# A Fourier stage whose standing operands are cut into two pieces of 64 columns, with two stores requested behind the loads

## The chip, the cores and the metric

The kernel runs on one core of a Trainium2 chip. The metric is the device time of one execution in microseconds (us); before the change it is 971.48 us, the median of three runs (970.88, 971.48 and 973.24). The core's engines are TensorE (PE in the profile, with its weight loads shown apart as PEld), VectorE (DVE), ScalarE (ACT), GpSimd (POOL) and SyncE (SP). In this kernel only SP requests transfers between the chip's memory (DRAM) and the core.

## The reference

One encoder layer over 256 prompt tokens and 2048 sample tokens, each 1024 wide, all in 32-bit floats:

```python
h = rms_norm(x, g_pre)
q, k, v, z_a, u_f, z_f = jnp.split(h @ w_in, [512, 1024, 1536, 2048, 2560], axis=-1)
y_a = neighbourhood_attention(q, k, v, rpb)      # 8 heads of 64, windows of 8 rows x 16 columns on a grid 64 wide
ug = u_f.reshape(b, s, 8, 64)
spec = jnp.fft.fft2(ug, axes=(1, 3), norm='ortho')       # over the tokens and the 64 channels of a group
y_f = spec.real.reshape(b, s, 512) @ w_f + b_f
mixed = concat([rms_norm(y_a, g_na) * silu(z_a), rms_norm(y_f, g_f) * silu(z_f)])
y = x + rms_norm(mixed @ w_out, g_post)
```

## The kernel before

The kernel is written as one long program; a scheduler, when it is compiled, sets the order of each engine's instructions, near the order of the code but not the same. Where the code says `tc.issue_after(x)`, what stands under it may not be issued ahead of `x`. Every tile comes from a pool, and a tile that takes over memory from another waits for that one's last reader or writer.

Its stages, in order: the input projections (the `mm` matmuls, 16 pairs of output blocks, `i` from 0 to 15; to 549 us); the Fourier stage's second step with its small products (549 to 576.6 us); the y stage, which multiplies the spectrum by the mixing weights (576.6 to about 606 us); the attention loop, into which the output projection is woven (to the end).

**The last pair of the projections.** Pair 15 gives two blocks of z (the gates' operand). Its function `store(f)` applies Silu on ScalarE (L882) to `o[f]`, a 128x1024 tile named `f`, and requests a store of 512 KB to `zD` (L883). Pair 15's stores are the last two.

**The Fourier stage's second step** (`stage2`, called at L1075). The tokens' transform is split in two; the first step's result lies in DRAM as `ZD` and comes back as `zg` tiles (`load_z`, L831), four of 128x512 for each of four quarter spectra `gq`. For each `gq` and each column group `c` from 0 to 4, `dft` (L1019) issues for four rows `g` a float32 matmul: its standing operand is columns of `zg`, its moving operand 64 columns of the table `d2` (`d_4717` and `d_4719` in the rows below). For `c` below 4 the standing operand is 128 columns wide; for `c` 4 it is three pieces of 32 columns, which write three bands of 32 rows of the result. The result is `pab`, 128 x 4 x 64 in PSUM. In `gq` 0 there is also a matmul with one moving column (`pny`), in `gq` 2 two with 129 moving columns from the upper table `f256`, whose standing operand is `up` (`pup`). `pab` rotates over three banks: two of tag b and one of tag c.

`split_ab` takes each result from PSUM as a rounded high part (a cast, by ScalarE at L1016, or by VectorE for `gq` 0 and `c` below 3) and a low part (VectorE's subtraction, L1017), in the tiles `abh` and `abl`; for `c` 4 these are L1031 and L1033.

`pq` (L1062) and `pq32` (L1069) make the standing operands of the y stage, `pqh`, `pql` and `w32`, from the tables `cs`, `c32` and the mixing weights `wf`; `pq(0)` stands behind `gq` 2, the others behind `gq` 3.

**The y stage** (`y_mm` and `y_out`). For each of four output blocks `e` and three token ranges `ti`, in the order 2, 0, 1, thirteen matmuls go into two PSUM tiles, `py1` and `py2`. ScalarE adds the bias (L1268), VectorE combines both into the tile `Y` (L1276), and `Y` is stored to `yD`, the first 256 tokens at L1302, the other 2048 (1 MB) at L1325. `Y` has two buffers, `py2` two and `py1` three. For the block `e` 3 the attention's first scores follow.

**The transfers.** SP issues its requests one after another, and each engine keeps the order it was compiled in. Beside the tables and `zg`, these are the attention's first keys `kl` (L1091), the bias tables `tb`, queries, values, gates, and eight pieces `wo1` of the output weights (L1234). The tiles `kl` lie in memory that earlier tiles held, among them pair 15's `f` tiles.

**Norm sums.** In the attention loop `norm_sums` adds squares over channels with a matmul into the PSUM tile `ptb`, copies the sums to the tile `nsb` (L1481, eight times in all) and `norm_turn` transposes it later. `ptb` is a pair of banks that two memsets clear once (L992).

Of the kernel before, what the change touches and what calls it, by code (L numbers as in the profile page):

```python
# [10 lines left out]
F32 = mybir.dt.float32  # L11
F32R = mybir.dt.float32r
AF = mybir.ActivationFunctionType
ALU = mybir.AluOpType
# [154 lines left out]
def build(tc, A, O):  # L169
    nc = tc.nc  # L170
# [6 lines left out]
    kD = dr.tile([4, 128, T], F32, name="kD")  # L177
# [3 lines left out]
    zD = dr.tile([2, 512, T], F32, name="zD")  # L181
# [23 lines left out]
    dnyq = cst.tile([128, 2], F32, name="dnyq")  # L205
# [512 lines left out]
    for c in range(3, 6):  # L718
# [7 lines left out]
        if c == 4:  # L726
# [33 lines left out]
    for b in range(16):  # L760
        kind, blk = divmod(b, 4)
# [73 lines left out]
    def load_d(j):  # L835
        return load([128, 8, 128], A["d2"][:, 8 * j:8 * j + 8, :], "d2")

    zgs = []
    for i in range(16):
        sg, pr = divmod(i, 8)  # L840
        if i == 8:
# [37 lines left out]
        def store(f):  # L879
            ts = slice(TP + 1024 * sg, TP + 1024 * sg + 1024)  # L880
            if kind < 2:
                silu_[0] = nc.scalar.activation(o[f], o[f], AF.Silu)  # L882
                nc.sync.dma_start(zD[kind, (blk + f) * 128:(blk + f) * 128 + 128, ts], o[f])  # L883
            else:
                nc.sync.dma_start((kD if kind == 2 else qD)[blk + f, :, ts], o[f])

        silu_ = [None]
        for j in range(7):
            if i in (0, 8):
                if j in (0, 3):  # L890
# [79 lines left out]
            else:  # L970
                comb(0, 1, "u4", p)
                store(0)
        if kind < 2:
            silu = silu_[0]

    man.close()
    with tc.issue_after(silu.ins):
        nc.scalar.preload_act_table_set("natural_log_exp_and_others")
    ph.close()


# [6 lines left out]
    sqs = sqp.tile([128, T], F32, name="sqs")  # L988
    ab = pf.enter_context(tc.tile_pool(name="ab", bufs=1))
    ptb = [ps.tile([128, 512], F32, tag="t", name="ptb", bufs=2) for i in range(2)]  # L990
    for x in ptb:
        nc.vector.memset(x, 0.0)  # L992
    pg = ExitStack()
    sm = pg.enter_context(tc.tile_pool(name="smF", bufs=1))
    f256 = sm.tile([128, 2, 258], F32, name="f256")
# [7 lines left out]
    nc.sync.dma_start(c32, A["c32"])  # L1003
    wf = sm.tile([128, 4, 512], F32, name="wf")
    nc.sync.dma_start(wf, A["wf"])

# [5 lines left out]
    a32 = ab.tile([96, NCOL], F32R, name="a32")  # L1012
    AC = [[x[:, c % 2] for x in AB[c // 2]] for c in range(4)]

    def split_ps(dh, dl, src, vec=False):
        nc.vector.tensor_copy(dh, src) if vec else nc.scalar.copy(dh, src)  # L1016
        nc.vector.tensor_tensor(out=dl, in0=src, in1=dh.bitcast(F32), op=ALU.subtract)  # L1017

    def dft(p, c, pairs):  # L1019
        sts = [(p[32 * r:32 * r + 32], slice(256, 512, 8)) for r in range(3)] if c == 4 else \  # L1020
            [(p, slice(c * 128, c * 128 + 128))]
        for out, cols in sts:
            for x, (z, d) in enumerate(pairs):
                nc.tensor.matmul(out, z[:, cols], d, start=x == 0, stop=x == len(pairs) - 1)  # L1024


    def split_ab(gq, c, view, p):
        if c < 4:
            split_ps(view(AC[c][0]), view(AC[c][1]), p, gq == 0 and c < 3)
        else:  # L1030
            nc.scalar.copy(view(a32), p)  # L1031
            lo = view(a32[64:96])
            nc.vector.tensor_tensor(out=lo, in0=p[64:96], in1=lo.bitcast(F32), op=ALU.subtract)  # L1033

    def stage2(gq, zg, c):
        m = int(c in (2, 3))
        np_ = 96 if c == 4 else 128
        x = (gq * 5 + c) % 3 == 2
        p = ps.tile([np_, 4, 64], F32, tag="c" if x else "b", name="pab", bufs=1 if x else 2)
        for g in range(4):  # L1040
            dft(p[:, g, :], c, [(zg[g], d2[gq // 2][:, (gq % 2) * 4 + g, m * 64:m * 64 + 64])])
        split_ab(gq, c, lambda a: a[:, :1024].rearrange("p (k q g l) -> p q g k l", k=16, q=4, g=4)[:, gq],
                 p.rearrange("p g (k l) -> p g k l", l=4))
        if gq == 0:
            p = ps.tile([np_, 1], F32, tag="a", name="pny")
            dft(p, c, [(zg[0], dnyq[:, m:m + 1])])
            split_ab(gq, c, lambda a: a[:, 1024:1025], p)
        if gq == 2:
            p = ps.tile([np_, 129], F32, tag="a", name="pup")
            dft(p, c, [(up[:, t], f256[:, t, 129 * m:129 * m + 129]) for t in range(2)])  # L1050
            split_ab(gq, c, lambda a: a[:, 1025:1154], p)
# [4 lines left out]
    def pq(m):  # L1056
        h = gt([128, 2, 512], F32R, "pqh")
        l = gt([128, 2, 512], F32R, "pql")
        for c in range(2):
            p = ps.tile([128, 512], F32, tag="a", name="ppq")  # L1060
            for x in range(2):
                nc.tensor.matmul(p[64 * x:64 * x + 64], cs2[:, m, :], wf[:, 2 * c + x, :], start=True, stop=True)  # L1062
            split_ps(h[:, c], l[:, c], p)
        PQ.append((h, l))
# [8 lines left out]
    for gq in range(4):  # L1073
        for c in range(5):
            stage2(gq, zgs[gq], c)  # L1075
        if gq == 2:
            pq(0)
    pq(1)
    pq32()
    pg.close()  # L1080
# [7 lines left out]

    def fetch_k(kk, pr, x):
        ts = slice(x * (T // 2), (x + 1) * (T // 2))  # L1090
        nc.sync.dma_start(kk[1][:, ts].bitcast(F32), kD[pr, :, ts])  # L1091

    def split_k(kk, x):
        ts = slice(x * KQ, (x + 1) * KQ)
# [124 lines left out]
    sc = load_k(0)  # L1219
    KK = {0: load_k(0)}  # L1220
    for x in range(2):
        fetch_k(KK[0], 0, x)
    for x in range(4):
        split_k(KK[0], x)
    load_t(0, 0)
    mask_p(0)
    for g in G[:2]:
        prep(g)
        prep_v(g)
    load_t(0, 1)  # L1230
    wo1 = [[gt([128, 2, 512], F32R, "wo1") for c in range(4)] for n in range(2)]
    for n in range(2):
        for c in range(4):
# [81 lines left out]
    for e in range(4):  # L1315
        Y = sqy.tile([128, T], F32, tag="Y", name="Y", bufs=2)
        if e < 3:
            for ti in (2, 0, 1):
                y_out(e, ti, *y_mm(e, ti))
                if e == 2 and ti == 2:  # L1320
                    nc.sync.dma_start(y0[:, 0, :3], yD[1, :3, :, :128].rearrange("c p t -> p c t"))
                    nc.sync.dma_start(y0[:, 1], zD[0, :, :128].rearrange("(c p) t -> p c t", p=128))
                if e == 2 and ti == 0:
                    nc.gpsimd.tensor_tensor(out=y0[:, 0, :3], in0=y0[:, 0, :3], in1=y0[:, 1, :3], op=ALU.mult)
            nc.sync.dma_start(yD[1, e, :, TP:], Y[:, TP:])  # L1325
            if e == 2:
                Y2 = Y
            for i in range(T // SQ if e < 2 else 1):
                ts = slice(i * SQ, i * SQ + SQ)
                if e == 0:  # L1330
                    nc.scalar.activation(sqs[:, ts], Y[:, ts], AF.Square)
                elif e == 2:
                    sq = sm.tile([128, SQ], F32, tag="sqf", name="sqf", bufs=2)
                    nc.scalar.activation(sq[:, :TP], Y[:, :TP], AF.Square)
                    nc.gpsimd.tensor_tensor(out=sqs[:, :TP], in0=sqs[:, :TP], in1=sq[:, :TP], op=ALU.add)
                else:
                    sq = sm.tile([128, SQ], F32, tag="sqf", name="sqf", bufs=2)
# [24 lines left out]
        split_q(G[2])  # L1362
        soft(G[1], 0)
        y_out(e, 1, *py)
# [111 lines left out]
    def norm_sums(sq, ts):  # L1476
        n = 32 * len(ts)
        for x, t in enumerate(ts):
            nc.tensor.matmul(ptb[0][32 * x:32 * x + 32, :128], ones32, sq[:, t * 128:t * 128 + 128], start=True, stop=True)
        o = sm.tile([128, 128], F32, name="nsb", bufs=1)[:n]  # L1480
        nc.scalar.copy(o, ptb[0][:n, :128])  # L1481
        nsb.append(o)

    def norm_turn(dst, ts):
# [298 lines left out]
```

## Time and profile before

| | |
|---|---|
| median of three runs | 971.48 us |
| the profiled execution | 970.48 us, its span 968.7 us |
| PE busy | 958.9 us, 99% of the span |
| DVE, ACT, POOL busy | 709.5, 497.5, 430.2 us |
| moved by transfers | 279.89 MB, 289 GB/s in the mean |

The profiled execution is shorter than the median by 1.0 us. A row of the profile's groups or its timeline names line, engine, operation, output and inputs, the shape and a count; a line that is a helper's, like L1024 for `dft`, stands for several callers, told apart by the tile names. A float32 matmul shows as two records. Line numbers are those of the kernel before; the changed kernel's are a few higher or lower.

### The profile page before, as it was taken

How to read it: one execution, taken by the hardware profiler on the slowest of the kernel's cores; microseconds unless marked ns; L12 is line 12 of the kernel's file. 1: busy time of each engine (PE TensorE's matmuls, PEld its weight loads, DVE VectorE, ACT ScalarE, POOL GpSimd, SP SyncE). 2: the span in 40 equal slices, each digit the busy share in tenths (PEclk: the TensorE clock that was granted, in tenths of full speed). 3: DMA queues.
4: the chain of work that ended last, by engine and by line, in shares of the span. 5: the costliest groups of instructions: out<-in, count | busy, mean ns of one | idle time of the engine just before them, and what ended most of it. 6: DMA issues, size and time to landing. Idle time of an engine off the chain costs nothing.

```text
span 968.7 us, 17031 instructions
## 1 busy us (share of the span) xinstructions
PE 958.9 (99%) x5769; PEld 801.0 (83%) x5769; DVE 709.5 (73%) x1306; ACT 497.5 (51%) x1078; POOL 430.2 (44%) x400
## 2 busy tenths in 40 slices
PE   9999999999999999999999999999999999999997
PEld 7889988888888888888888879887788888878886
DVE  6768987777986867787777446776665656649997
ACT  6836675433325533333344255677666776744443
POOL 3100003464752202756654033577677686624544
PEclk9999999999999999999999999999999999999999
DMA  9899696556849996599989898698887998979993
GB/s 327 312 373 357 234 366 240 194 189 252 318 163 377 352 410 239 211 371 320 322 303 339 301 328 300 210 281 273 258 240 234 286 327 270 296 244 331 330 346 129
DMA packets 146450, 279.89 MB, mean 289 GB/s; under 512 B 13162, under 2 KB 84284, under 8 KB 142972
## 3 DMA queue, kind: packets, MB, share of 16 engines
q1 hardware_dynamic: 145932, 278.41, 82.4%
q8 instruction: 46, 0.75, 0.3%
q10 hardware_dynamic: 432, 0.39, 0.1%
q14 instruction: 40, 0.33, 0.1%
HBM read 184.37 MB, written 101.72 MB: 295 GB/s over the span
## 4 chain that ended last, share of the span: by engine, by line
PE 96%; DVE 1%; ACT 1%; issue 1%; POOL 1%; DMA 0%; DVEq 0%; SPq 0%; POOLq 0%; ACTq 0%
PE po L1432 19%; PE mm L165 18%; PE mm L164 18%; PE mm L166 18%; PE pv L1521 5%; PE ptb L1505 5%; PE s L1181 4%; PE pab L1024 2%; PE py L164 1%; PE py L166 1%; PE py L165 1%; DMA gpre<-gpre 0%; PE ppq L1062 0%; PE pz L166 0%; PE pz L164 0%
## 5 line engine op out<-in xcount | busy, mean ns | idle before, releaser
L164 PE MATMUL mm<-xh,wa 128*128 128x512 f32 x448 | 174.4, 389 | 0.0
L165 PE MATMUL mm<-xl,wa 128*128 128x512 f32 x448 | 174.3, 389 | 0.0
L166 PE MATMUL mm<-xh,wa 128*128 128x512 f32 x448 | 174.3, 389 | 0.0
L536 POOL TENSOR_TENSOR ws<-wr 128x512 f32<-128x512 f32 x16 | 22.2, 1386 | 226.6 <-DMA wr<-wz 222.8
L1215 POOL TENSOR_SCALAR w<-w,m 128x480 f32<-128x480 f32 (+6 forms) x136 | 86.0, 644 | 46.3 <-DVE m L1212 35.9
L164 PEld LDWEIGHTS mm<-xh,wa 128*128 128x128 f32 x448 | 84.1, 188 | 17.6
L166 PEld LDWEIGHTS mm<-xh,wa 128*128 128x128 f32 x448 | 84.1, 188 | 17.5
L165 PEld LDWEIGHTS mm<-xl,wa 128*128 128x128 f32 x448 | 84.1, 188 | 17.4
L1432 PE MATMUL po<-wo,yh 128*128 128x512 f32 x272 | 90.4, 413 | 0.0
L551 DVE TENSOR_TENSOR wa<-wr,wa 128x512 fp32r<-128x512 f32 x60 | 68.5, 1149 | 27.1 <-ACT wa L550 26.8
L1208 ACT ACTIVATE w<-w,m 128x480 f32<-128x480 f32 (+6 forms) x136 | 79.3, 586 | 17.1 <-DVE m L1203 17.1
L1432 PE MATMUL po<-w,yh 128*128 128x512 f32 x280 | 86.7, 391 | 0.0
L1203 DVE CUSTOM_DVE_ANT_1 w<-s,tb 128x360 f32<-128x360 f32 (+5 forms) x124 | 62.4, 541 | 10.3 <-PE s L1181 9.8
L589 POOL TENSOR_TENSOR mt<-mt,rmask 128x880 f32<-128x880 f32 (+2 forms) x24 | 51.0, 2139 | 34.1 <-DVE mt L585 27.6
L165 PE MATMUL mm<-vl,xh 128*128 128x512 f32 x168 | 65.5, 390 | 0.2 <-DVE vl L482 0.2
L164 PE MATMUL mm<-vh,xh 128*128 128x512 f32 x168 | 65.4, 389 | 0.0
L166 PE MATMUL mm<-vh,xl 128*128 128x512 f32 x168 | 65.4, 389 | 0.0
L877 DVE TENSOR_TENSOR f<-u,mm 128x512 f32<-128x512 f32 x64 | 43.5, 680 | 28.0 <-PE mm L166 23.1
L1432 PEld LDWEIGHTS po<-w,yh 128*128 128x128 f32 x280 | 52.3, 188 | 10.9 <-issue 0.2
L1505 PE MATMUL ptb<-ident,w 128*120 128x128 f32 (+5 forms) x428 | 59.5, 276 | 1.0 <-ACT nsb L1481 0.9
L550 ACT CAST wa<-wr 128x512 fp32r<-128x512 f32 x60 | 36.4, 617 | 44.1 <-PE mm L166 23.2
L1521 PEld LDWEIGHTS pv<-pt,v 120*64 120x64 f32 (+6 forms) x896 | 48.2, 136 | 12.8 <-issue 9.6
(263 smaller groups left out, 2394.3 us busy)
## 6 DMA issues: line engine op xcount, KB each, us to landing
wr<-wz SPq DMA_DIRECT2D x48, 512.0 KB
vl<-sD SPq DMA_DIRECT2D x20, 512.0 KB
xm<-xm SPq DMA_DIRECT2D x9, 1024.0 KB
oD<-ofs SPq DMA_DIRECT2D x18, 512.0 KB
of<-oD SPq DMA_DIRECT2D x18, 512.0 KB
yr<-yD SPq DMA_DIRECT2D x34, 256.0 KB
zD<-f SPq DMA_DIRECT2D x16, 512.0 KB
woD<-wo SPq DMA_DIRECT2D x16, 512.0 KB
```

Source lines behind the costliest of these rows:

```text
L164: nc.tensor.matmul(out, lh, rh, start=first, stop=False)
L165: nc.tensor.matmul(out, lh, rl, start=False, stop=False)
L166: nc.tensor.matmul(out, ll, rh, start=False, stop=last)
L551: nc.vector.tensor_tensor(out=o[:, 1], in0=src, in1=o[:, 0].bitcast(F32), op=ALU.subtract)
L589: nc.gpsimd.tensor_tensor(out=o, in0=i, in1=rmask[:, m0:m0 + n].unsqueeze(2).to_broadcast([128, n, 80]), op=ALU.add)
L877: nc.vector.tensor_tensor(out=dst(f, b), in0=src(uu[u]), in1=src(p), op=op)
L1203: nc.vector.tensor_tensor_reduce(out=rows(g["w"][b][:, h, :n], w), in0=rows(g["s"][2 * b + h][:, :n], w), in1=tv, scale=1.0, scalar=3.0e38 ...
L1208: nc.scalar.activation(w, w, AF.Exp, bias=m[:, h:h + 1], scale=-1.0, accum_out=m[:, 2 + h:3 + h])
L1215: nc.gpsimd.tensor_scalar(w, w, m[:, 4 + h:5 + h], 1.0, ALU.mult, ALU.mult)
L1432: nc.tensor.matmul(p, (d["l"] if x == 2 else d["h"])[:, c], w(n, int(x == 1), c), start=j == 0, stop=j == 11)
L1505: nc.tensor.transpose(ptb[h][:nk, j * 128:j * 128 + 128], g["w"][b][:, h, c0:c0 + nk], ident)
L1521: nc.tensor.matmul(p[hs, b], g["v"][:nk, v, hs], g["pt"][b][:nk, h, j * 128:j * 128 + 128], start=j == 0, stop=j == len(ch) - 1)
```

## The change

The change does five things.

1. `dft` gets a width. For `pab` and `pny` with `c` below 4 the standing operand goes in as two pieces of 64 columns, which write the upper and the lower 64 rows of the result. `pup` keeps 128, and `c` 4 its three pieces of 32.
2. The last pair's two stores are not requested in `store` but kept in the list `late` and requested behind the loads of `f256`, `up`, the last `zg`, `cs`, `c32` and `wf`. The Silus stay where they were. Code behind `issue_after(put.ins)`, `put` being the request for the second half of `kl`, holds the order of the requests that follow.
3. ScalarE's load of the table of functions goes from behind the last Silu to behind the last cast of `gq` 3. VectorE's two memsets of `ptb` go behind `gq` 1.
4. In `gq` 0 the cast for `c` 2 goes from VectorE to ScalarE.
5. The eight copies to `nsb` go from ScalarE to VectorE.

```diff
         def store(f):
             ts = slice(TP + 1024 * sg, TP + 1024 * sg + 1024)
             if kind < 2:
-                silu_[0] = nc.scalar.activation(o[f], o[f], AF.Silu)
-                nc.sync.dma_start(zD[kind, (blk + f) * 128:(blk + f) * 128 + 128, ts], o[f])
+                nc.scalar.activation(o[f], o[f], AF.Silu)
+                late.append((zD[kind, (blk + f) * 128:(blk + f) * 128 + 128, ts], o[f]))
+                if i < 15:
+                    nc.sync.dma_start(*late.pop())
...
     man.close()
-    with tc.issue_after(silu.ins):
-        nc.scalar.preload_act_table_set("natural_log_exp_and_others")
...
-    for x in ptb:
-        nc.vector.memset(x, 0.0)
...
     nc.sync.dma_start(wf, A["wf"])
+    for d, t in late:
+        nc.sync.dma_start(d, t)
...
-    def dft(p, c, pairs):
-        sts = [(p[32 * r:32 * r + 32], slice(256, 512, 8)) for r in range(3)] if c == 4 else \
-            [(p, slice(c * 128, c * 128 + 128))]
+    def dft(p, c, pairs, w=128):
+        if c == 4:
+            sts = [(p[32 * r:32 * r + 32], slice(256, 512, 8)) for r in range(3)]
+        else:
+            sts = [(p[r:r + w], slice(c * 128 + r, c * 128 + r + w)) for r in range(0, 128, w)]
...
-            split_ps(view(AC[c][0]), view(AC[c][1]), p, gq == 0 and c < 3)
+            split_ps(view(AC[c][0]), view(AC[c][1]), p, gq == 0 and c < 2)
...
-            dft(p[:, g, :], c, [(zg[g], d2[gq // 2][:, (gq % 2) * 4 + g, m * 64:m * 64 + 64])])
+            dft(p[:, g, :], c, [(zg[g], d2[gq // 2][:, (gq % 2) * 4 + g, m * 64:m * 64 + 64])], 64)
...
-            dft(p, c, [(zg[0], dnyq[:, m:m + 1])])
+            dft(p, c, [(zg[0], dnyq[:, m:m + 1])], 64)
...
             stage2(gq, zgs[gq], c)
+        if gq == 1:
+            with tc.issue_after(last["dve"].ins):
+                for x in ptb:
+                    nc.vector.memset(x, 0.0)
         if gq == 2:
             pq(0)
+        if gq == 3:
+            with tc.issue_after(last["act"].ins):
+                nc.scalar.preload_act_table_set("natural_log_exp_and_others")
...
-        fetch_k(KK[0], 0, x)
+        put = fetch_k(KK[0], 0, x)
...
-        nc.scalar.copy(o, ptb[0][:n, :128])
+        nc.vector.tensor_copy(o, ptb[0][:n, :128])
```

Three places show what moves on the engines; rows give line, operation, tiles and sizes, with a count at the end where several alike stand in a row. The first is SP, from the loads of `zg` to the keys `kl`; before:

```order
L831 DMA zg<-ZD 128x512 x12
L883 DMA zD<-f 128x1024 x2
L996 DMA f_4859<-f 128x516
L998 DMA up<-uD 128x2x512
L831 DMA zg<-ZD 128x512 x4
L1001 DMA cs_4869<-cs 128x128
L1003 DMA c_4871<-c 128x384
L1005 DMA wf<-wf 128x2048
L1091 DMA kl<-kD 128x1152 x2
```

and after:

```order
L831 DMA zg<-ZD 128x512 x12
L990 DMA f_4854<-f 128x516
L992 DMA up<-uD 128x2x512
L831 DMA zg<-ZD 128x512 x4
L995 DMA cs_4864<-cs 128x128
L997 DMA c_4866<-c 128x384
L999 DMA wf<-wf 128x2048
L1001 DMA zD<-f 128x1024 x2
L1102 DMA kl<-kD 128x1152 x2
```

The two `zD` stores stood between the first twelve `zg` and `f256`; they now stand between `wf` and `kl`.

The second is TensorE from the last `pny` of `gq` 0 to the first groups of `gq` 2; before:

```order
L1024 MATMUL pny<-dnyq,zg 128x1
L1024 MATMUL pab<-d_4717,zg 32x64 x12
L1024 MATMUL pny<-dnyq,zg 32x1 x3
L1024 MATMUL pab<-d_4717,zg 128x64 x16
L1024 MATMUL pab<-d_4717,zg 32x64 x12
L1024 MATMUL pab<-d_4719,zg 128x64 x4
L1024 MATMUL pup<-f_4859,up 128x129 x2
L1024 MATMUL pab<-d_4719,zg 128x64 x4
```

and after:

```order
L1028 MATMUL pny<-dnyq,zg 64x1 x2
L1028 MATMUL pab<-d_4717,zg 32x64 x12
L1028 MATMUL pny<-dnyq,zg 32x1 x3
L1028 MATMUL pab<-d_4717,zg 64x64 x32
L1028 MATMUL pab<-d_4717,zg 32x64 x12
L1028 MATMUL pab<-d_4719,zg 64x64 x8
L1028 MATMUL pup<-f_4854,up 128x129 x2
L1028 MATMUL pab<-d_4719,zg 64x64 x8
```

Each matmul with 128 standing columns has become two with 64, except `pup`'s, so that in `gq` 2 the two widths take turns.

The third is ScalarE from the products of `pq(0)` to `w32`, and after the change the first bias of the y stage; `kh` is the cast of the keys, `qh` that of the queries. Before:

```order
L1016 CAST pqh<-ppq 128x512
L1095 CAST kh<-kl 128x576
L1016 CAST pqh<-ppq 128x512
L1016 CAST abh_4875<-pab 128x4x16x4 x2
L1016 CAST abh_4877<-pab 128x4x16x4
L1095 CAST kh<-kl 128x576 x2
L1016 CAST abh_4877<-pab 128x4x16x4
L1095 CAST kh<-kl 128x576
L1031 CAST a_4879<-pab 96x4x16x4
L1016 CAST pqh<-ppq 128x512 x2
L1163 CAST qh<-ql 128x256 x2
L1070 CAST w_4880<-ppq 96x512
```

and after:

```order
L1017 CAST pqh<-ppq 128x512 x2
L1017 CAST abh_4872<-pab 128x4x16x4 x2
L1017 CAST abh_4874<-pab 128x4x16x4 x2
L1035 CAST a_4876<-pab 96x4x16x4
L1088 ACT_TABLE_LOAD
L1017 CAST pqh<-ppq 128x512 x2
L1106 CAST kh<-kl 128x576 x4
L1074 CAST w_4877<-ppq 96x512
L1281 ACTIVATE t_5294<-py_5279,bfs 128x386
```

The load of the table stands behind the last cast of `gq` 3 (before, it stood behind the last Silu, ahead of these rows). The casts of the keys, which were spread between those of `gq` 3, stand together behind the last `pqh`, and `w32` comes ahead of the queries' casts.

More of the change, by code (lines that the diff above doesn't have):

```diff
@@ L836, in load_d @@
         return load([128, 8, 128], A["d2"][:, 8 * j:8 * j + 8, :], "d2")
-    zgs = []
+    zgs, late = [], []
     for i in range(16):
@@ L881, in store @@
             if kind < 2:
-                silu_[0] = nc.scalar.activation(o[f], o[f], AF.Silu)
-                nc.sync.dma_start(zD[kind, (blk + f) * 128:(blk + f) * 128 + 128, ts], o[f])
+                nc.scalar.activation(o[f], o[f], AF.Silu)
+                late.append((zD[kind, (blk + f) * 128:(blk + f) * 128 + 128, ts], o[f]))
+                if i < 15:
+                    nc.sync.dma_start(*late.pop())
             else:
                 nc.sync.dma_start((kD if kind == 2 else qD)[blk + f, :, ts], o[f])
-        silu_ = [None]
         for j in range(7):
@@ L972, in build @@
                 store(0)
-        if kind < 2:
-            silu = silu_[0]
     man.close()
-    with tc.issue_after(silu.ins):
-        nc.scalar.preload_act_table_set("natural_log_exp_and_others")
     ph.close()
@@ L1013, in build @@
     AC = [[x[:, c % 2] for x in AB[c // 2]] for c in range(4)]
+    last = {}
     def split_ps(dh, dl, src, vec=False):
-        nc.vector.tensor_copy(dh, src) if vec else nc.scalar.copy(dh, src)
-        nc.vector.tensor_tensor(out=dl, in0=src, in1=dh.bitcast(F32), op=ALU.subtract)
-    def dft(p, c, pairs):
-        sts = [(p[32 * r:32 * r + 32], slice(256, 512, 8)) for r in range(3)] if c == 4 else \
-            [(p, slice(c * 128, c * 128 + 128))]
+        if vec:
+            nc.vector.tensor_copy(dh, src)
+        else:
+            last["act"] = nc.scalar.copy(dh, src)
+        last["dve"] = nc.vector.tensor_tensor(out=dl, in0=src, in1=dh.bitcast(F32), op=ALU.subtract)
+    def dft(p, c, pairs, w=128):
+        if c == 4:
+            sts = [(p[32 * r:32 * r + 32], slice(256, 512, 8)) for r in range(3)]
+        else:
+            sts = [(p[r:r + w], slice(c * 128 + r, c * 128 + r + w)) for r in range(0, 128, w)]
         for out, cols in sts:
@@ L1028, in split_ab @@
         if c < 4:
-            split_ps(view(AC[c][0]), view(AC[c][1]), p, gq == 0 and c < 3)
+            split_ps(view(AC[c][0]), view(AC[c][1]), p, gq == 0 and c < 2)
         else:
-            nc.scalar.copy(view(a32), p)
+            last["act"] = nc.scalar.copy(view(a32), p)
             lo = view(a32[64:96])
@@ L1090, in fetch_k @@
         ts = slice(x * (T // 2), (x + 1) * (T // 2))
-        nc.sync.dma_start(kk[1][:, ts].bitcast(F32), kD[pr, :, ts])
+        return nc.sync.dma_start(kk[1][:, ts].bitcast(F32), kD[pr, :, ts])
     def split_k(kk, x):
@@ L1221, in build @@
     for x in range(2):
-        fetch_k(KK[0], 0, x)
+        put = fetch_k(KK[0], 0, x)
     for x in range(4):
         split_k(KK[0], x)
-    load_t(0, 0)
+    with tc.issue_after(put.ins):
+        load_t(0, 0)
     mask_p(0)
[L1227 to L1230, printed above, removed]
+    with tc.issue_after(put.ins):
+        for g in G[:2]:
+            prep(g)
+            prep_v(g)
+        load_t(0, 1)
     wo1 = [[gt([128, 2, 512], F32R, "wo1") for c in range(4)] for n in range(2)]
@@ L1321, in build @@
                     nc.sync.dma_start(y0[:, 0, :3], yD[1, :3, :, :128].rearrange("c p t -> p c t"))
-                    nc.sync.dma_start(y0[:, 1], zD[0, :, :128].rearrange("(c p) t -> p c t", p=128))
+                    with tc.issue_after(put.ins):
+                        nc.sync.dma_start(y0[:, 1], zD[0, :, :128].rearrange("(c p) t -> p c t", p=128))
                 if e == 2 and ti == 0:
```

## The prediction

> **What bounds the kernel now.** I read the page's busy shares and clock first, then the chain that ended last.
>
> ```profile
> PE 958.9 (99%) x5769; PEld 801.0 (83%) x5769; DVE 709.5 (73%) x1306; ACT 497.5 (51%) x1078; POOL 430.2 (44%) x400
> PEclk9999999999999999999999999999999999999999
> PE 96%; DVE 1%; ACT 1%; issue 1%; POOL 1%; DMA 0%; DVEq 0%; SPq 0%; POOLq 0%; ACTq 0%
> ```
>
> TensorE is busy 99% of 968.7 us at the full clock and makes 96% of the chain, so removing TensorE time helps at once, unless something that was hidden close behind it then sets the pace. Next I read the edited stage by form, as weight loads one after another, and by windows (the first four are quarter spectra 0, 1 with the start of 2, the rest of 2, and 3; the fifth is the y stage up to the place that matters below).
>
> ```profile
> L1024 PE MATMUL pab<-d,zg 128*128 128x64 f32 x128 | 15.9, 275 | 0.0
> L1024 PE MATMUL pab<-d,zg 128*32 128x64 f32 x96 | 2.9, 232 | 0.0
> ...
> 548.90:554.31 5.41, 5.41 (x72) 5.33 (x71) 4.37 (x15) 2.77 (x4) 0.00 (x0) 1.00 0.68 243
> 554.31:559.15 4.84, 4.84 (x66) 4.71 (x61) 2.48 (x9) 2.25 (x7) 0.00 (x0) 1.00 1.06 375
> 559.15:565.40 6.25, 6.25 (x83) 5.96 (x82) 3.18 (x9) 2.96 (x10) 0.00 (x0) 1.00 1.01 406
> 567.26:571.64 4.38, 4.38 (x59) 4.24 (x57) 2.46 (x5) 3.10 (x8) 1.83 (x2) 1.00 0.84 214
> 576.62:595.22 18.60, 18.60 (x106) 18.36 (x105) 9.11 (x39) 9.32 (x21) 4.51 (x7) 1.00 0.99 352
> ```
>
> Columns after each window are its length, busy time of PE, PEld, DVE, ACT and POOL, the clock, DMA share and GB/s. PE never rests in any of them, while VectorE and ScalarE rest about half the time: the second step is TensorE's. The DMA column is as telling: around 1.0 in three of the five, so transfers are nearly a second bound.
>
> **The halves.** A plain matmul here is two records. Rows of weight loads give the pace:
>
> ```profile
> 560.02 0.97 PEld L1024 LDWEIGHTS pab<-d,zg 128*128 128x128 f32 x8
> 560.91 0.53 PEld L1024 LDWEIGHTS pup<-f,up 128*128 128x128 f32 x4
> ...
> 553.58 0.59 PEld L1024 LDWEIGHTS pab<-d,zg 128*32 128x32 f32 x24
> 554.08 0.22 PEld L1024 LDWEIGHTS pny<-dnyq,zg 128*32 128x32 f32 x6
> 554.31 0.19 PEld L1024 LDWEIGHTS pab<-d,zg 128*128 128x128 f32 x1
> ...
> 804.94 0.14 PEld L1521 LDWEIGHTS pv<-pt,v 80*64 80x64 f32 x2 [0.35 <-issue]
> 804.94 0.85 PEld L1521 LDWEIGHTS pv<-pt,v 80*64 80x64 f32 x16 [0.35 <-issue]
> ```
>
> Eight 128-column records take 560.91 − 560.02 = 0.89 us, 111 ns each. Twenty-four 32-column ones take 554.08 − 553.58 = 0.50 us, three side by side every 62 ns. No row has 64 columns with 64 moving ones; the nearest are attention's pv rows, 64 columns with 128 moving: two loads in 0.14 us where one alone lasts as long, sixteen in 0.85 us, so pairs run side by side at about 106 ns. Bounds for a pair of halves: 62 ns (as the 32-column triples) and 106 to 111 (no gain). I take 62, since the moving size is the same as in the triples.
>
> All 128 large pab records would save 128 × 49 ns = 6.3 us. Three things keep that from being whole. In quarter 2 each pab group stands between pup matmuls that keep 128 columns, so the array goes from one width to the other twice per column group. What a change of width costs is seen after the 32-column pny: its two triples should be over about 0.1 us after 554.08, the next load starts at 554.31, so about 0.13 us. Column group of quarter 2: 0.89 + 0.45 = 1.34 now, 0.50 + 0.45 + 2 × 0.13 = 1.21 after, a gain of 0.1 each, bounds 0 and 0.2, taken 0.05: 0.2 in all. In quarters 0, 1 and 3 the evacuation comes close:
>
> ```profile
> 550.13 1.03 DVE L992 MEMSET ptb<- 128x512 f32 x2
> 551.06 0.40 DVE L1016 CAST abh<-pab 128x256 fp32r<-128x256 f32 x1
> 551.50 0.42 DVE L1017 TENSOR_TENSOR abl<-pab,abh 128x256 fp32r<-128x256 f32 x1
> 551.91 0.41 DVE L1016 CAST abh<-pab 128x256 fp32r<-128x256 f32 x1
> 551.13 1.28 ACT L978 ACT_TABLE_LOAD   x1
> 555.45 0.37 ACT L1016 CAST abh<-pab 128x256 fp32r<-128x256 f32 x1 [0.65 <-PE pab L1024]
> ```
>
> A piece is filled in 0.50 us, cast by ScalarE in 0.37 and subtracted by VectorE in 0.42. A bank is held for 0.50 + 0.37 + 0.42 and some 0.4 of hand-overs, 1.7 us; three banks make 0.57 us a piece instead of 0.50. Quarter 1: 32 × 49 ns = 1.6 less 0.3, so 1.3. Quarter 0: 1.8, as its eight pny records shorten too; there two groups are cast and subtracted by VectorE at 551.91 − 551.06 = 0.85 us each, but the memsets of 1.03 us that stood ahead have gone behind quarter 1, and ScalarE takes the third group because its 1.28 us table load has gone. Quarter 3: 1.0, as ScalarE's two casts of pq(0) stand at its start. The table load is now behind quarter 3's last cast, beside pq(1) and pq32; kh's casts follow it, then w32, which by this replay arrives as the y stage asks for it. Sum: 1.8 + 1.3 + 0.2 + 1.0 = 4.3 us that TensorE enters the y stage earlier (bounds 3.5 and 4.9 where halves overlap, 0 and below where not).
>
> **The stores, and where the gain stops.** SP is the one queue of transfers; it issues in order and a waiting transfer holds all behind it. SP's rows, four narrow windows and the row that VectorE waits on:
>
> ```profile
> 548.47 2.98 SPq L883 DMA_DIRECT2D zD<-f  x2
> 551.55 0.38 SPq L996 DMA_DIRECT2D f<-f  x1
> 556.58 1.33 SPq L1091 DMA_DIRECT2D kl<-kD  x2
> 585.41 0.33 SPq L1325 DMA_DIRECT2D yD<-Y  x1
> ...
> 548.47:548.97 0.50, 0.50 (x4) 0.42 (x3) 0.00 (x0) 0.00 (x0) 0.00 (x0) 1.00 0.00 0
> 548.97:549.47 0.50, 0.50 (x6) 0.46 (x5) 0.14 (x1) 0.00 (x0) 0.00 (x0) 1.00 0.55 197
> 550.47:550.97 0.50, 0.50 (x6) 0.50 (x6) 0.44 (x2) 0.50 (x1) 0.00 (x0) 1.00 0.23 82
> 570.00:572.50 2.50, 2.50 (x38) 1.84 (x39) 0.98 (x3) 2.31 (x6) 1.29 (x1) 1.00 0.73 176
> 572.50:591.50 19.00, 19.00 (x97) 16.04 (x94) 9.20 (x32) 9.23 (x22) 6.56 (x7) 1.00 1.00 349
> ...
> 594.21 1.34 DVE L1276 TENSOR_TENSOR Y<-t,py 128x252 f32<-128x252 f32 x7 [2.00 <-DMA yD<-Y]
> ...
> 596.44 0.34 PE L164 MATMUL py<-abh,pqh 128*128 128x384 f32 x1
> 549.33 0.69 DVE L877 TENSOR_TENSOR f<-u,mm 128x512 f32<-128x512 f32 x1 [2.03 <-PE mm L166]
> ```
>
> Y has two buffers, so the third output block may not be combined until the first block's store, requested at 585.41, has landed; VectorE sits idle 2.0 us for it until 594.21. That store queues behind a transfer system full from 572.5 on, so asking earlier does not land it earlier. The combines end at 594.21 + 1.34 = 595.55; py has two buffers of that tag, and the block's next such matmul starts at 596.44. With 0.05 us to hand over, TensorE is only 0.84 us from waiting for that store. Of the 4.3 us, whatever exceeds 0.84 becomes one idle stretch of TensorE there.
>
> How the landing moves (δ): f256 is requested when the last mm ends, 549.4 instead of the first store's 548.47, so transfers start 0.9 later. Between the stores the system lies nearly idle from 550.5 to 552.0, about 1.3 us, since the second waits for ScalarE's silu; the loads fill that: −1.3. But kl takes over the memory of the stored tiles and now waits for both landings, and ten or more requests behind it wait too. The system runs dry. No row shows such a hole; a request's start shows 0.7 us from issue to data (548.47 to the middle of the second window), and the upper end is the 2.2 us made of start plus that 1.5 us idle stretch. I take 1.2, nearer the start. The hole at 570 to 572.5, 27% of 2.5 us = 0.7, may fill as the wo loads find wf's memory free earlier: 0 to −0.7, taken −0.3. δ = 0.9 − 1.3 + 1.2 − 0.3 = +0.5, ends −0.4 and +1.8. The stage's gain that survives is 0.84 − 0.5 = 0.3 us, ends 1.2 and −1.0. wf itself comes earlier, and the stores' readers only at the attention stage.
>
> **The norm sums.** Eight copies move from ScalarE to VectorE:
>
> ```profile
> L1481 ACT COPY nsb<-ptb x8: 247/260/261, 630.0 to 858.1; 128x128 f32<-128x128 f32 x6, 64x128 f32<-64x128 f32 x2
>   PE ptb L1505: 0.9, 1
>   PEld ptb L1505: 0.6, 2
> ...
> 629.68 0.39 ACT L1537 ACTIVATE ysq<-pv 128x256 f32<-128x256 f32 x1 [1.16 <-DVE y L1535]
> 629.96 0.25 ACT L1481 COPY nsb<-ptb 64x128 f32<-64x128 f32 x1
> ```
>
> TensorE waited 1.5 us in three places for them, the copy standing behind a square that waits for VectorE. On VectorE it has no such square ahead, but pushes the softmax maxima back 0.26 us each, covered by VectorE's 27% of rest. I take half, 0.8, ends −0.5 and 1.5.
>
> **Sum.** 0.3 + 0.8 = 1.1 us. The profiled execution took 970.48 us (span 968.7 and what lies around it), 1.0 below the median of 971.48; I subtract from the median: 970.4, own range 968.8 to 973.0.
>
> **Rivals.**
> *The whole gain comes through.* The first store lands 3.5 us earlier too, because the quicker stage frees memory earlier and the queue has less idle time than I count. For it: holes of 1.3 and 0.7 us exist; against: together they are too short, and the share is 1.00 for 19 us. Time: 971.5 − 4.3 − 0.8 = 966.4.
> *Halves do not overlap.* If each half passes alone at 62 ns, a pair costs 125 against 111: 128 × 14 ns = +1.8, and seven more changes of width +0.9; with the norm sums −0.8 it ends at 973.4. It is slower by over 0.3% from a pair of 133 ns on (128 × 22 ns + 0.9 − 0.8 = 2.9); at 222, halves as long as wholes, 985. Against it stand triples and pv pairs.
> *The idle stretch slows the clock.* TensorE would rest 4.0 us at the third block, longer than anywhere in this trace, and may come back at a reduced clock; the clock row shows no reduction, with no such rest to cause it. At half rate for about the same length it costs 2 us: 970.4 + 2 = 972.4. The Trainium skill, "TensorE: Matmul & The Clock Gate", section "Why this matters for your kernels", says gaps above about 3 us send the array back to half clock until it has been busy a while; by its window of 3.4 us the loss is an estimated 1.7 us. No run here shows it yet.
>
> The Trainium skill's "TensorEngine Tiling (Array Packing)", "Key Properties", has a change of tiling mode drain the engine, which speaks against halves between pup groups; the 0.13 us above agrees in kind. By its "up to 2×" a pair would take an estimated 56 ns, which would make the stage's gain 0.6 larger and the time, by the store, the same.
>
> **Chances.** Store gates it 0.60; whole gain 0.22; clock falls 0.08; no overlap 0.10, of which 0.05 reaches beyond 133 ns. What this measurement can tell from no change is about 0.3%, 2.9 us. Faster 0.24 (the whole gain and a little of the first case's edge), same 0.70, slower 0.06. The range runs from the whole gain's 966.3 to 973.2, leaving out the worst overlap and store cases.
>
> **What would show it.** After: pab loads of 64 columns in pairs every 62 ns; the y stage beginning near 572.3; one TensorE wait of 3 to 4 us, for VectorE's Y combine, behind a DMA yD wait on VectorE far longer than 2.0 us, with the store landing near 594.7; kl issued only at about 562; no nsb wait on PE. I am wrong if the y stage starts late (overlap), if the yD wait is short (the store moved), or if the clock row dips after the rest.

## The result, and the profile after

| | before | after |
|---|---|---|
| median of seven runs each, us | 971.67 (970.88 to 974.57) | 977.35 (976.31 to 983.5) |
| ratio of the times, 95% interval | | 1.0063 (1.0039 to 1.0087) |
| span of the profiled execution, us | 968.7 | 975.4 |
| mean granted clock | 0.998 | 0.993 |

The kernel became slower by 5.7 us; 970.4 had been forecast, with a range up to 973.2. The page of the changed kernel answers to the first three lines of the prediction (busy shares, granted clock, chain by engine; the fourth is the chain by line):

```profile
PE 956.3 (98%) x5905; PEld 796.8 (82%) x5905; DVE 707.3 (73%) x1312; ACT 497.0 (51%) x1072; POOL 431.1 (44%) x400
...
PEclk9999999999999999999999997999999999999999
...
PE 92%; DMA 4%; DVE 1%; issue 1%; POOL 1%; ACT 0%; SPq 0%; DVEq 0%; POOLq 0%; ACTq 0%
PE po L1446 20%; PE mm L165 18%; PE mm L166 18%; PE mm L164 18%; PE pv L1535 5%; PE ptb L1519 5%; PE s L1192 4%; DMA wo<-woD 1%; DMA zD<-f 1%; DMA yD<-Y 1%; DMA kl<-kD 1%; PE py L164 0%; PE pab L1028 0%; DMA gpre<-gpre 0%; PE py L165 0%
```

TensorE's busy time fell by 2.6 us while the span grew by 6.7. Transfers had no share of the chain and now have 4%, and the chain names them; in the order of time they are `zD`, `kl`, `wo` and `yD`, with casts and the first y matmuls between `kl` and `wo`. One slice of the clock row reads 7.

TensorE's waits between 549 and 615 us, of which the kernel before had none, and its timeline (start, length, what; the time it sat idle before and until what, in brackets):

```profile
PE py L164 <- DVE Y L1289: 8.5, 1, 8.5
PE py L1276 <- DVE w L1075: 0.6, 1, 0.6
PE pab L1028 <- DVE abl L1018: 0.3, 1, 0.3
...
549.36 0.69 PE L1028 MATMUL pab<-d,zg 128*64 128x64 f32 x16
549.87 0.23 PE L1028 MATMUL pny<-dnyq,zg 128*64 128x1 f32 x4
...
571.78 0.74 PE L164 MATMUL py<-abh,pqh 128*128 128x386 f32 x1
...
592.37 0.34 PE L1276 MATMUL py<-a,w 96*128 96x384 f32 x1
601.16 0.66 PE L164 MATMUL py<-abh,pqh 128*128 128x384 f32 x1 [8.46 <-DVE Y L1289]
601.62 0.52 PE L165 MATMUL py<-abl,pqh 128*128 128x384 f32 x1
601.94 0.52 PE L166 MATMUL py<-abh,pql 128*128 128x384 f32 x1
...
606.33 0.33 PE L164 MATMUL py<-abh,pqh 128*128 128x386 f32 x1
606.50 0.34 PE L165 MATMUL py<-abl,pqh 128*128 128x386 f32 x1
```

The halves did what was forecast: eight pairs of them take 549.87 − 549.36 = 0.51 us, 64 ns a pair, and the y stage begins 4.8 us earlier on the clock of the trace. Then TensorE rests 8.5 us in the third output block, at the place foreseen. Behind the rest the matmuls start every 320 ns instead of every 170, until about 606.2.

The queue's side: SP's wait, its timeline, narrow windows (after the window and its length: busy time of PE, PEld, DVE, ACT and POOL, clock, DMA share, GB/s), and VectorE's row for the combine.

```profile
SPq L1102 <- DMA zD<-f: 9.3, 2, 8.1
...
549.46 0.33 SPq L990 DMA_DIRECT2D f<-f  x1
555.38 0.97 SPq L1001 DMA_DIRECT2D zD<-f  x2
565.67 0.80 SPq L1102 DMA_DIRECT2D kl<-kD  x2
590.67 0.33 SPq L1339 DMA_DIRECT2D yD<-Y  x1
...
562.00:562.50 0.50, 0.50 (x4) 0.19 (x4) 0.50 (x2) 0.24 (x1) 0.00 (x0) 1.00 1.14 451
563.50:564.00 0.50, 0.50 (x16) 0.38 (x14) 0.41 (x1) 0.23 (x2) 0.00 (x0) 1.00 0.05 16
565.00:565.50 0.50, 0.18 (x8) 0.04 (x2) 0.50 (x3) 0.41 (x2) 0.00 (x0) 1.00 0.02 8
565.50:566.00 0.50, 0.47 (x16) 0.47 (x16) 0.50 (x2) 0.10 (x1) 0.00 (x0) 1.00 0.00 0
567.00:567.50 0.50, 0.50 (x4) 0.14 (x2) 0.26 (x2) 0.48 (x2) 0.00 (x0) 1.00 0.59 111
...
596.00:600.00 4.00, 0.00 (x0) 0.00 (x0) 0.33 (x1) 0.00 (x0) 0.00 (x0) 0.50 1.00 412
...
599.67 2.34 DVE L1289 TENSOR_TENSOR Y<-t,py 128x252 f32<-128x252 f32 x10 [11.37 <-DMA yD<-Y]
```

SP stood still from 556.4 to 565.67 for the landing of the two stores. The bulk of their data was through by about 562.75 (the share from 562.5 to 563 is 0.57); from 563.5 to 565.5 the share is 0.02 to 0.06, about a sixteenth, as if one of the sixteen DMA engines were still at work, and `kl` could be asked for only when that one had finished. Nothing moves from 565.5 to 566.5. Everything behind `kl` came late with it, the first Y block's store too: the combine that waits for it starts at 599.67 instead of 594.21, and VectorE sat 11.4 us for it.

To keep out the time at which the stage begins (548.9 to 553.8 us in the traces below, also between kernels that do not differ ahead of it), I count from the first weight load of a `pab` matmul. Three stretches then hold the rest of the program: to the first weight load of a y matmul, from there to that of the first output product `po`, and from there to the end.

| us | stage | y stage | rest | sum |
|---|---|---|---|---|
| before | 27.7 | 29.8 | 362.3 | 419.8 |
| after | 22.4 | 41.8 | 361.9 | 426.1 |
| difference | −5.3 | +11.9 | −0.4 | +6.3 |

Of the 11.9 us, 8.5 are the rest, 1.0 the wait for `w32` in the first output block with the gap about it (574.11 to 575.09 in the timeline), and 2.4 the slow clock: from the first matmul behind the rest to the first `po` it is 12.4 us, against 10.0 before. The wait for `w32` comes from the late `kl` too. On ScalarE the casts of the keys stand ahead of the cast of `w32`:

```profile
571.26 2.58 ACT L1106 CAST kh<-kl 128x576 fp32r<-128x576 f32 x4 [1.58 <-issue]
573.75 0.58 ACT L1074 CAST w<-ppq 96x512 fp32r<-96x512 f32 x1
```

The stage's gain depends a little on where one cuts. In the four kernels with 128 columns the first `pab` load starts with the last matmul of the projections, in the nine with halves 0.3 us behind it (549.35 and 549.04 in the changed kernel). Counted from that matmul, the stage gains 5.0 us instead of 5.3.

### The profile page after: what moved, and what is told of

The parts are those of the page before. It is cut to its first block, busy times and chain, and to the rows that moved or that the text cites. A ratio compares the mean times of both kernels' runs of the same rounds, so it can differ in the third digit from the quotient of the medians.

```text
span 975.4 us, 17307 instructions
## 1 busy us (share of the span) xinstructions
PE 956.3 (98%) x5905; PEld 796.8 (82%) x5905; DVE 707.3 (73%) x1312; ACT 497.0 (51%) x1072; POOL 431.1 (44%) x400
## 4 chain that ended last, share of the span: by engine, by line
PE 92%; DMA 4%; DVE 1%; issue 1%; POOL 1%; ACT 0%; SPq 0%; DVEq 0%; POOLq 0%; ACTq 0%
PE po L1446 20%; PE mm L165 18%; PE mm L166 18%; PE mm L164 18%; PE pv L1535 5%; PE ptb L1519 5%; PE s L1192 4%; DMA wo<-woD 1%; DMA zD<-f 1%; DMA yD<-Y 1%; DMA kl<-kD 1%; PE py L164 0%; PE pab L1028 0%; DMA gpre<-gpre 0%; PE py L165 0%
## 5 line engine op out<-in xcount | busy, mean ns | idle before, releaser
L536 POOL TENSOR_TENSOR ws<-wr 128x512 f32<-128x512 f32 x16 | 22.9, 1433 | 228.1 <-DMA wr<-wz 222.7
```

## The experiments

The table gives, for each kernel, the timed ratio to the kernel before and, from its one trace, the three stretches, the landing of the first Y block's 1 MB store counted from the first `pab`, and TensorE's longest rest in the y stage or ahead of the first output tiles.

| kernel | ratio, 95% interval | stage | y stage | rest of program | store lands | longest rest |
|---|---|---|---|---|---|---|
| before | | 27.7 | 29.8 | 362.3 | 45.2 | none |
| after | 1.0063 (1.0039, 1.0087) | 22.4 | 41.8 | 361.9 | 50.2 | 8.5 |
| e1 stores early | 0.9997 (0.9985, 1.0009) | 25.1 | 31.5 | 362.6 | 45.0 | 1.5 |
| e2 128 columns | 1.0048 (1.0031, 1.0064) | 27.7 | 36.6 | 362.1 | 50.6 | 4.5 |
| e3 filled rest | 1.0047 (1.003, 1.0063) | 22.7 | 38.5 | 362.0 | 49.5 | 0.6 |
| e4 filled queue | 1.0005 (0.9992, 1.0017) | 22.9 | 37.1 | 362.2 | 45.6 | 4.3 |
| e5 wo late | 1.005 (1.0038, 1.0062) | 22.9 | 36.6 | 364.8 | 38.2 | 3.1 |
| e6 filled queue, wo late | 1.0003 (0.9994, 1.0011) | 22.4 | 33.6 | 363.7 | 36.4 | 3.1 |
| e7 stores early, wo late | 1.0018 (1.0009, 1.0026) | 24.9 | 32.2 | 363.8 | 39.0 | 2.0 |
| e8 before, nsb on VectorE | 1.0007 (0.9999, 1.0016) | 27.7 | 29.8 | 362.6 | 45.3 | none |
| e9 filled queue, half of wo late | 0.9993 (0.9982, 1.0004) | 22.4 | 29.9 | 365.4 | 40.6 | 1.4 |
| e10 the same, behind the second block | 1.0019 (1.0006, 1.0032) | 22.4 | 34.2 | 363.8 | 39.6 | 4.0 |
| e11 before, half of wo late | 1.0018 (1.0006, 1.003) | 27.7 | 29.8 | 364.2 | 40.4 | 0.7 |

**e1: the stores where they were.**

```diff
-                if i < 15:
-                    nc.sync.dma_start(*late.pop())
+                nc.sync.dma_start(*late.pop())
```

> The changed kernel with the two zD stores requested where they were before, ahead of f256; everything else of the change stays. Store theory (kl waits for the landing of the stores, the transfers run dry, the first Y block's store lands 5.5 us late): the wait of SP for zD is gone, the first yD store lands near 594 us again, TensorE's idle stretch at the third block shrinks from 8.5 to about 4 us; 970 to 971 us if the clock holds over 4 us of rest, up to 973 if it falls. Halves theory (the early arrival of TensorE alone makes the loss): no better than 976.

Measured 0.9997, no change from before. The store lands as before and the rest is 1.5 us, not 4, as the stage gained only 2.5 us: its own waits give the reason.

```profile
PE ppq L1065 <- DVE a L1036: 1.6, 1, 1.6
PE py L164 <- DVE Y L1288: 1.5, 1, 1.5
PE pup L1027 <- DMA up<-uD: 0.9, 1, 0.9
PE pab L1027 <- DVE abl L1017: 0.5, 1, 0.5
```

The late stores thus are worth 2.8 us within the stage, and cost more behind it. The clock did not fall after 1.5 us of rest.

**e2: 128 columns again, stores late.**

```diff
-            dft(p[:, g, :], c, [(zg[g], d2[gq // 2][:, (gq % 2) * 4 + g, m * 64:m * 64 + 64])], 64)
+            dft(p[:, g, :], c, [(zg[g], d2[gq // 2][:, (gq % 2) * 4 + g, m * 64:m * 64 + 64])])
...
-            dft(p, c, [(zg[0], dnyq[:, m:m + 1])], 64)
+            dft(p, c, [(zg[0], dnyq[:, m:m + 1])])
```

> The changed kernel with 128 standing columns for pab and pny as before; the stores stay behind wf. Store theory: the first yD store still lands near 599.5 us and TensorE goes on near 601 us as in the changed kernel, having come 5 us later to that place, so it rests about 3.6 us; 975 us if the clock holds, 977 if it falls. Halves theory: 971 to 972 us, as before the change.

Measured 1.0048: the loss without the halves. The store lands as late as in the changed kernel, TensorE comes 4.3 us later to it (it begins the y stage 5.3 us later but does not wait for `w32`) and rests 4.5 us instead of 8.5, and the clock fell. The halves change how long TensorE waits, not when it goes on. The stage takes 27.7 us, as before the change, although the moved casts, memsets, table load and stores are in: its gain needs the halves.

**e3: the rest filled with work.**

```diff
         for m, p in ((0, p1), (1, p2)):
+            if (e, ti, m) == (2, 1, 1):
+                pd = ps.tile([128, 512], F32, tag="c", name="warm", bufs=1)
+                for x in range(45):
+                    nc.tensor.matmul(pd[:, :384], PQ[0][0][:, 0, es_], AB[0][0][:, 0, cs], start=True, stop=True)
```

> The changed kernel with 45 additional matmuls of 384 columns, whose result nobody reads, in the place where TensorE rests 8.5 us (7.8 us of work at full clock, so they end before the wait does). Clock theory (the rest itself makes the clock fall to 0.5 and that costs 2.2 us behind it): the granted clock stays at 1.00, py matmuls behind the wait start every 174 ns, 975 us. Rival (the slow rows behind the wait come from the transfers or from PSUM, not from the rest): 977.3 us and 320 ns a matmul as in the changed kernel.

```profile
599.67 0.51 PE L1275 MATMUL warm<-abh,pqh 128*128 128x384 f32 x2
600.76 0.41 PE L164 MATMUL py<-abh,pqh 128*128 128x384 f32 x1 [0.58 <-DVE Y L1293]
601.01 0.33 PE L165 MATMUL py<-abl,pqh 128*128 128x384 f32 x1
601.18 0.34 PE L166 MATMUL py<-abh,pql 128*128 128x384 f32 x1
...
600.00:602.00 2.00, 1.42 (x9) 1.27 (x8) 1.61 (x9) 0.42 (x1) 0.74 (x1) 1.00 0.38 131
```

The same wait stands at the same place, but the matmuls behind it start every 170 to 180 ns and the clock reads 1.00; from the first of them to the first `po` it takes 10.1 us, as before the change, and not 12.4. So the slow rows come from the rest. In the trace this is worth 2.3 us in that piece; the timed ratios of this kernel and the changed one, 1.0047 and 1.0063, point the same way, but their intervals overlap.

**e4: requests ahead of the keys.** The code of `load_t(0, 0)` and of the loop over `G[:2]` stands ahead of the loop with `fetch_k`:

```diff
+    load_t(0, 0)
+    for g in G[:2]:
+        prep(g)
+        prep_v(g)
     for x in range(2):
         put = fetch_k(KK[0], 0, x)
...
-    with tc.issue_after(put.ins):
-        load_t(0, 0)
     mask_p(0)
     with tc.issue_after(put.ins):
-        for g in G[:2]:
-            prep(g)
-            prep_v(g)
         load_t(0, 1)
```

> The changed kernel, stores late, but the loads of the first bias table, and of queries, values and gates of the first two groups, are requested ahead of the keys kl, so that requests stand in the queue while the stores land. Store theory (what costs is the dry queue, not the place of the stores): no hole of 4 us in the transfers near 563 to 567 us, the first yD store lands 3 to 5 us sooner, near 595 to 597; 971 to 974 us. Rival (the late stores cost by themselves, as traffic in a full system): within 1 us of 977.

Measured 1.0005. The stores are as late as in the changed kernel, and yet:

```profile
563.00:568.00 5.00, 4.18 (x86) 2.80 (x79) 2.78 (x7) 2.77 (x7) 0.00 (x0) 1.00 1.03 418
...
PE py L164 <- DVE Y L1288: 4.3, 1, 4.3
```

The system stays full where it ran dry, and the first Y store lands 4.6 us sooner, at 45.6. Against the kernel before it is 0.4 late. So the dry queue behind SP's wait, not the place of the stores as such, is nearly all of the delay. The 4.3 us of rest that remain are the stage's gain, eaten at the gate; the clock fell after it too.

**e5, e6, e7: the eight wo loads behind the first Y block's store**, in the changed kernel, in e4, and in e1:

```diff
-    for n in range(2):
-        for c in range(4):
-            nc.sync.dma_start(wo1[n][c].bitcast(F32),
-                              woD[1, :, c, :, n * 512:n * 512 + 512].rearrange("x p d -> p x d"))
...
             nc.sync.dma_start(yD[1, e, :, TP:], Y[:, TP:])
+            if e == 0:
+                for n in range(2):
+                    for c in range(4):
+                        nc.sync.dma_start(wo1[n][c].bitcast(F32),
+                              woD[1, :, c, :, n * 512:n * 512 + 512].rearrange("x p d -> p x d"))
```

> The changed kernel, stores late, but the eight wo loads (4 MB) are requested behind the first Y block's store instead of ahead of it. Store theory (the third block waits for a store that queues behind these loads): the first yD store lands near 588 us, well before it is asked for; no rest of TensorE at the third block, clock 1.00; the stage's 5.3 us come through unless the y loads, now behind the wo loads, make a new wait ahead of the output products: 966 to 970 us. Rival (the dry queue of 563 to 567 us delays all transfers, so some later wait takes the place of the one removed): 973 us or more.

> Both: first bias table, queries, values and gates ahead of the keys, and the wo loads behind the first Y block's store; halves and late stores as in the changed kernel. Store theory: no dry queue and no gate at the third block; 966 to 969 us. Rival (transfers as a whole bound this stretch, so what is not waited for at the third block is waited for at the output products): no faster than 971.

> Stores where they were before the change, halves, and the wo loads behind the first Y block's store. The stage gained 2.5 us with the stores early (the loads of up and wf come later there) against 5.3 with them late; without the gate at the third block this 2.5 comes through: 969 to 970 us. If 5.3 comes through, 967; if the gate was not the only limit, 971.5 or more.

The rivals won: 1.005, 1.0003, 1.0018. The first store does land 11 to 14 us sooner than in the changed kernel, and the rest moves on to the output products, which need the y loads, now behind 4 MB of wo. In e6 (TensorE's wait, and GpSimd's row for the y tile):

```profile
PE po L1446 <- ACT y0h L1364: 3.1, 1, 3.1
...
604.79 0.99 POOL L1333 TENSOR_TENSOR y<-y 128x384 f32<-128x384 f32 x1 [9.26 <-DMA y<-yD]
```

In e5 TensorE also waited 3.1 us at the fourth block, whose buffer waits for the second block's store, and that one queues behind the wo loads.

**e8: the kernel before, nsb on VectorE.**

```diff
-        nc.scalar.copy(o, ptb[0][:n, :128])
+        nc.vector.tensor_copy(o, ptb[0][:n, :128])
```

> The kernel before with the eight nsb copies on VectorE and nothing else changed. The prediction's term: 0.8 us faster (ends 0.5 slower, 1.5 faster). The parts from the first output product to the end in the traces so far (361.9 to 362.6 us with the copies on VectorE, 362.3 without) rather say 0.0 to 0.4 us, not to be told from no change.

Measured 1.0007: the forecast gain is not there. Who waited for `nsb` in this kernel:

```profile
  POOL w L1215: 2.2, 2
  ACT dl L1378: 1.3, 1
  PE ptb L1505: 0.6, 1
  PEld ptb L1505: 0.2, 1
```

TensorE's waits went from 1.5 to 0.8 us, and GpSimd's from 1.0 to 2.2.

**e9, e10, e11: half of the wo loads later.** In e9 (on e4) and e11 (on the kernel before) the four loads of the second half are requested with the third block's y loads:

```diff
-    for n in range(2):
+    for n in range(1):
         for c in range(4):
             nc.sync.dma_start(wo1[n][c].bitcast(F32),
...
                         nc.sync.dma_start(y0[:, 1], zD[0, :, :128].rearrange("(c p) t -> p c t", p=128))
+                for c in range(4):
+                    nc.sync.dma_start(wo1[1][c].bitcast(F32),
+                          woD[1, :, c, :, 512:1024].rearrange("x p d -> p x d"))
```

In e10 (on e4) they stand behind the second Y block's store.

> Halves, stores late, first table, queries, values and gates ahead of the keys; of the eight wo loads four stay and the other four are requested beside the third block's y loads. Transfer theory (the order of the queue decides what TensorE waits for; 2 MB less stand ahead of the first Y block's store, and the y loads have only Y stores ahead of them): that store lands 5.4 us sooner than with all eight ahead, no rest at the third block nor at the output products, clock 1.00, the stage's 5 us come through: 966 to 968 us. Rival (the stretch is bound by bytes moved, so a wait of 2 us or more appears somewhere behind): 971 us or more.

> As the run before, but the four later wo loads behind the second Y block's store, ahead of the y loads. Transfer theory: no rest at the third block; the y loads come behind 2 MB of wo, some 5 us later than in the run before, so TensorE rests 1 to 3 us ahead of the output products: 969 to 972 us. Rival: no different from the run before.

> The kernel before, 128 columns, stores early, with only the second half of the wo loads moved to the third block's y loads. Transfer theory: TensorE did not wait for the store in the kernel before (0.8 us to spare), so nothing is gained: within 0.2% of before. Rival (the order of the wo loads is worth time by itself and not only what it lets through): 1 us faster or more.

In e9 the y stage runs in 29.9 us, without a rest, behind a stage of 22.4: the gain of the halves stands at the first `po` in full, 5.3 us. Then the rest of the program takes 3.1 us longer than before the change, 2.4 of them in TensorE's waits at the next output tile (the two shown and one of 0.3):

```profile
PE po L1448 <- ACT ofs L1477: 1.4, 1, 1.4
PE ptb L1521 <- ACT pt L1523: 0.7, 1, 0.7
...
614.69 1.27 POOL L1425 TENSOR_TENSOR y<-y 128x512 f32<-128x512 f32 x1 [5.40 <-DMA y<-zD]
```

The next y loads stand behind the moved wo loads. From the first `pab` to the end e9's trace is 2.1 us shorter than that of before; timed, it is 0.9993, an interval that holds no change: its rival's 971 us or more came, not 966 to 968. It beats the changed kernel, not surely the kernel before. e10 makes TensorE rest 4.0 us for the y loads, more than the 1 to 3 expected, and its time too lies above the 969 to 972 expected. In e11 nothing is gained, as the transfer theory said, and the rival is out; at 1.0018, with an interval above 1, it rather loses 0.2%. The rest of its program is 1.9 us longer, of which TensorE's wait of 0.7 us at `ptb` stands at the same place as in e9. That part of what e9 lost behind `po` comes with the later wo loads fits this, but is not shown.

## Why the prediction was wrong

**The halves: right, a little undersized.** 64 ns a pair against 62; the stage gained 5.3 us (5.0 from the last projection matmul) where 4.3 (3.5 to 4.9) was summed. `w32` did not come as it was asked for but about 1 us late, behind the casts of the late `kl`.

**The gate: right place, wrong time.** That TensorE would be stopped at the third block by the landing of the first Y store was so, and e1 and e4 show it holds whatever the stores do. The step that failed is δ, the shift of that landing: +0.5 us, ends −0.4 and +1.8; VectorE's row moved by 5.5. Within it the failed term is the hole behind the stores, taken as 1.2 us with an upper end of 2.2. The narrow windows show it from 562.75 to beyond 566.5, some 3.7 us, and e4, which fills it, brings the store back by 4.6. Read the same way, e2, e3 and e5, which have the same wait, show 2.7 to 3.0 us, still above the upper end; where the landing's delay beyond the hole comes from was not separated. In the changed kernel the hole is longer than a request's start because SP waits for the last of the sixteen DMA engines, which by the share of a sixteenth ran about 2 us behind the others in that trace. The upper end was made of two idle stretches of the kernel before, neither of which contained such a landing. They were nearest in kind, but they were no bound. The −1.3 us for the gap between the stores did not come either: from 549.4 to 551.0 the share was only 0.26, the loads' own start.

**The clock: a rival of 0.08 that happened.** Its price, 2 us, was about right (2.4 by the trace, 2.3 by e3); its chance was far too low, since in my own likeliest case TensorE rested 4.0 us, and rests of 4.3 and 4.5 us in e4 and e2 were enough. The rule of the Trainium skill ("TensorE: Matmul & The Clock Gate", "Why this matters for your kernels") that I had set beside it agrees with these, and should have raised that chance: the two cases were one. The last section shows that shorter rests can do it too.

**The norm sums: wrong.** 0.8 us was forecast, e8 measured 1.0007 (0.9999 to 1.0016). TensorE's waits for the copy halved, as supposed, but GpSimd's doubled, and the program's end did not move.

**The other rivals.** Halves that do not overlap did not occur. The whole gain would have needed a store 3.5 us sooner; e9 had it 4.6 sooner and got the gain as far as the first `po`. The 985 us for halves as long as wholes should be 986 by its own terms.

The sum, as it stands after the result, by the trace's three stretches: −5.3 in the stage, +8.5 rest, +1.0 for `w32`, +2.4 clock, −0.4 behind: 6.2 of the 6.3 us. The prediction had −4.3, about +4.0 and −0.8.

## What to carry to other kernels

Before moving a store back in an in-order queue, look for the request that takes over the stored tile's memory: from that request on the whole queue waits for the landing, and the cost is the time until the last DMA engine is done plus a cold start, unless other requests stand between. When a shorter stage meets a gate that does not move, the saved time turns into one rest of TensorE, and a rest of some microseconds costs something more by the clock behind it (2.4 us here behind 8.5); add both before calling a hidden gain harmless. Where transfers are full for 40 us, reordering them chooses who waits: look at the second and third reader of the queue, not only at the one that waited first.

## What the runs showed of the hardware

Between 549 and 620 us the granted clock fell to 0.50 after rests of 2.0, 3.1, 4.0, 4.3, 4.5 and 8.5 us, and did not after 0.6 and 1.4 to 1.6. Length alone does not decide it. Away from the program's end the clock stood at 0.50 for 3.41, 6.83 or 10.24 us, which is one, two or three times 3.41, and in each of the nine traces with more than one fall, the falls lie a whole number of 3.41 us apart. So by these traces the clock is set anew at the ends of fixed steps of 3.41 us. The shortest of these rests that did it, in e7, and then windows cut at those steps, first of e7, then of e8 near the start of the program, then of e10:

```profile
605.17 0.34 PE L166 MATMUL py<-abh,pql 128*128 128x384 f32 x1
607.51 2.42 PE L1446 MATMUL po<-wo,y0h 128*128 128x512 f32 x6 [2.00 <-ACT y0h L1364]
...
605.30:608.71 3.41, 1.41 (x6) 0.72 (x5) 1.22 (x6) 0.95 (x3) 1.26 (x2) 1.00 0.01 2
608.71:612.12 3.41, 3.41 (x10) 2.56 (x9) 1.98 (x9) 3.01 (x10) 2.06 (x6) 0.50 0.53 154
612.12:615.53 3.41, 3.41 (x21) 2.75 (x20) 2.90 (x14) 1.71 (x5) 3.12 (x5) 1.00 0.52 214
...
4.19:7.60 3.41, 1.99 (x11) 1.30 (x11) 1.42 (x3) 2.00 (x5) 0.00 (x0) 1.00 0.96 340
7.60:11.01 3.41, 3.41 (x10) 2.63 (x9) 3.09 (x6) 2.58 (x7) 0.00 (x0) 0.50 1.00 329
...
604.48:607.89 3.41, 1.85 (x11) 1.52 (x9) 1.29 (x4) 0.00 (x0) 0.00 (x0) 1.00 0.76 276
607.89:611.30 3.41, 0.97 (x3) 0.55 (x4) 0.99 (x4) 0.94 (x2) 1.03 (x2) 1.00 0.01 4
```

In e7's first step TensorE was busy 1.41 us, so it idled 2.0 of 3.41, and the clock fell at the step's end, 1.2 us after TensorE was back at work. In e8 1.42 us of idle time sufficed. In e10 1.56 us did not, and the next step's 2.44 us did. Among all other whole steps at full clock in the thirteen traces, none with up to 1.46 us of idle time was followed by a fall, and each from 1.69 us on was. So the limit lies near 1.5 us of idle time within one step, and a rest of 2 us can do it or not, as the steps happen to cut it. Falls like e8's, in e4 and e9, also lie in the first 11 us, ahead of the stretches compared above. The Trainium skill ("TensorE: Matmul & The Clock Gate", "Why this matters for your kernels") puts the limit at gaps above about 3 us; these traces show it lower.
